# A hybrid decoder layer on Trainium2: building the order of instructions with and without a timed play-through

## The chip, the core and the metric

The kernel runs on one core of a Trainium2 chip. A core has a matrix engine (TensorE, PE in the rows, with its weight loads as PEld), a vector engine (VectorE, DVE), a scalar engine (ScalarE, ACT), a general engine (GpSimd, POOL) and SyncE (SP), which here issues nearly all transfers between the device's memory and the core's. Each engine works through its own list of instructions, and semaphores make one list wait for another. The metric is the device time of one execution in microseconds (us), as the median of several runs.

## The reference, cut to what matters

One layer of a decoder on 2048 prompt tokens and 8 sample tokens, 1024 wide. Two kinds of heads run beside each other between two norms, then an MLP follows.

```python
def _layer(x, states, params):
    h = _rmsnorm(x, norm_pre_mix)
    mix, new_states = _mixer(h, ...)          # h @ w_in, two head groups, o @ w_out
    x = x + _rmsnorm(mix, norm_post_mix)
    u = jnp.square(jax.nn.relu(_rmsnorm(x, norm_pre_mlp) @ w_up))
    return x + _rmsnorm(u @ w_down, norm_post_mlp), new_states

# group A: gated DeltaNet, chunk after chunk (the state S goes from one to the next)
    w_v = triangular_solve(A, bc * vc); w_k = triangular_solve(A, bc * exp(G) * kc)
    def step(S, xs):
        U = wv_ - wk_ @ S
        o = eg_ * (q_ @ S) + qk_ @ U
        return ge_ * S + ke_.T @ U, o
# group B: mLSTM, chunk after chunk (C, n and the running maximum m go on)
        num = w_prev * (q_ @ C) + (P * qk_) @ v_
        h = num / max(|den|, exp(-mt))
        C = w_prev_end * C + (p_end * k_).T @ v_
```

The outputs of both groups are normalised, gated, put side by side and multiplied with w_out. All states come back too.

## The kernel before, in words

The 2048 prompt tokens are worked on in four segments of 512 (the 8 sample tokens ride with the second, whose matmuls are 260 columns wide instead of 512). Each segment goes through the input projection (w_a, 28 units), the mixer, the output projection (w_o), two norms and the MLP (w_up, w_dn). Everything is float32. A product is made from three passes: weights and activations are split into a high and a low part, and hi x hi (L195), hi x lo (L196) and lo x hi (L200) are added in one PSUM bank (tile bk). A unit of weights is a Half, 128 x 512 numbers: SP loads it (L171, tile wraw, four buffers), ACT casts the high part (L178, tile whl, three buffers), DVE subtracts to get the low part (L183), PE runs 12 matmuls on it, and ACT or DVE takes the bank away.

The mixer is a chain of small steps that go between engines. One half of a segment's DeltaNet part (gdn_half, two chunks) does this: transposes (L520, L529) with squares on ACT (L525, L531), products of q and k (L563), a row-by-row solve on DVE (L596, L598) between two trips through memory, then for each chunk PE L618, ACT copies L622, PE L627, DVE L631 and L632, PE L636, ACT L638, PE L643, DVE L645; then for each chunk PE L655, DVE L658, PE L663, ACT L665 (tile W, one buffer), PE L672 with DVE L675 for the next state, PE L680 and L681 for the output, squares on ACT (L684), DVE L685, a power on POOL (L224), the scaling on ACT (L690) and the transposes of the result (L702 in out_T), which go to memory as dO. The mLSTM chunk (ml_chunk, four a segment) is a like chain: L718, L737, L746 and L747, L755, L764, L702, L770. Before the output projection, b_prep reads dO back (L1099). The means of the norms are made by squares on ACT (L1140), additions on POOL (L1141), a matmul (L1153), a power on POOL and a matmul that spreads the result (L1166).

The program writes the wide matmuls in a fixed list and lets the mixer and the norms run beside them: play() keeps an account of wide work and takes a step of such a stream (up to its next yield) when the account allows:

```python
            h.go(part)
            if streams:
                state["due"] += h.cost() * state["rate"]
                while streams and state["due"] > 0:
                    state["due"] -= step()
```

That is the program's order. It isn't yet the order on the engines: the framework (tile) takes every instruction with its place in the program as its priority (split() of a Half gets 300 places ahead of its own), plays the program through on a model of the core, and gives each engine the ready instruction with the best priority at that moment; buffers of a pool are handed out in the same play. What is not ready then is passed by what is. The result is a fixed list for each engine. In the kernel before, the model plays with an estimated time for each instruction (schedule_with_timeline_sim=True, L1586), so an instruction that must wait for another engine is passed by as many others as fit into the estimated wait. The mixer's steps, the splits and the loads all get their places in this way.

## Time and profile before

| what | value |
|---|---|
| median of 3 runs | 2667.09 us (2652.25 to 9010.13) |
| the profiled execution, its own time | 2654.11 us |
| span from its first to its last instruction | 2652.3 us |
| PE busy | 2599.9 us (98%) |
| DVE, ACT, POOL busy | 1727.5, 1283.5, 433.3 us (65%, 48%, 16%) |
| mean clock granted to PE | 0.996 of full speed |
| chain that ended last | PE 88%, DVE 4%, DMA 4%, issue 2%, ACT 1% |
| moved | 377.40 MB, mean 142 GB/s |

Busy times are sums over the span of one execution. A wait is idle time of an engine together with what ended it. The chain that ended last is followed back from the last instruction, at each step to what released it. Busy time of PE is modelled at its ends, so neighbouring matmuls overlap in it and a duration of one is taken from the distance of rows.

### The profile page before, as it was taken

To read this page: it belongs to the slowest core of one execution; us is meant where nothing else is said; L and a number is where in the kernel's file an instruction comes from. 1 tells how busy PE (TensorE), PEld (TensorE's weight loads), DVE (VectorE), ACT (ScalarE), POOL (GpSimd) and SP (SyncE) were. 2 spreads that over 40 slices of the span, in tenths; PEclk is the share of its full clock that TensorE was granted. 3 is DMA by queue.
4 is the path that set the end of the run, shared out by engine and by line. 5 is a ranking of instruction groups with operands and counts; after the bars stand their busy time and mean duration, and the time that the engine had idled before them with its cause. 6 is when DMAs were issued, how large, how long until landed. Compare 5 with 4: busy or idle time off the path is not lost.

```text
span 2652.3 us, 44344 instructions
## 1 busy us (share of the span) xinstructions
PE 2599.9 (98%) x15912; PEld 2268.5 (86%) x15912; DVE 1727.5 (65%) x3513; ACT 1283.5 (48%) x3120; POOL 433.3 (16%) x494
## 2 busy tenths in 40 slices
PE   8999999999999999999999999999999999999998
PEld 6879999787888788878899999997787888788887
DVE  7665758647747656774775766577758566765445
ACT  5636557435536345653655444466354355433332
POOL 2101112311000000530100000054000003552002
PEclk9999999999999999999999999999999999999999
DMA  5444457654324345754433343455333346565222
GB/s 173 155 147 144 151 152 222 207 156 134 108 92 126 96 141 167 236 186 135 139 97 110 107 141 119 138 173 163 99 112 112 106 144 205 182 197 147 93 96 84
DMA packets 292221, 377.40 MB, mean 142 GB/s; under 512 B 42325, under 2 KB 147785, under 8 KB 291993
## 3 DMA queue, kind: packets, MB, share of 16 engines
q1 hardware_dynamic: 289312, 365.13, 44.2%
q0 software_dynamic: 2688, 9.44, 1.3%
q8 instruction: 126, 2.06, 0.3%
q14 instruction: 95, 0.77, 0.1%
HBM read 314.04 MB, written 60.53 MB: 141 GB/s over the span
## 4 chain that ended last, share of the span: by engine, by line
PE 88%; DVE 4%; DMA 4%; issue 2%; ACT 1%; POOL 0%; SPq 0%; DVEq 0%; ACTq 0%; POOLq 0%
PE bk L195 26%; PE bk L196 26%; PE bk L200 26%; DMA wraw<-w_o 1%; DVE whl L183 1%; DVE nt L1214 1%; DMA xt<-x_prompt 1%; DVE X L1218 1%; DMA xt<-dO 1%; PE mx L563 1%; PE mx L655 1%; PE mx L770 1%; PE mx L680 1%; PE mx L681 1%; PE mx L747 1%
## 5 line engine op out<-in xcount | busy, mean ns | idle before, releaser
L178 ACT CAST whl<-wraw 128x512 fp32r<-128x512 f32 x872 | 539.4, 620 | 933.7 <-PE bk L200 866.3
L183 DVE TENSOR_TENSOR whl<-wraw,whl 128x512 fp32r<-128x512 f32 (+1 forms) x872 | 636.3, 732 | 447.5 <-ACT whl L178 433.3
L195 PE MATMUL bk<-Y,whl 128*128 128x512 f32 (+2 forms) x2208 | 733.9, 347 | 4.2 <-ACT whl L178 2.0
L196 PE MATMUL bk<-Y,whl 128*128 128x512 f32 (+2 forms) x2208 | 732.1, 346 | 0.0
L195 PE MATMUL bk<-X,whl 128*128 128x512 f32 (+3 forms) x2024 | 654.9, 340 | 7.2 <-ACT whl L178 7.1
L196 PE MATMUL bk<-X,whl 128*128 128x512 f32 (+3 forms) x2024 | 653.5, 339 | 2.7 <-DVE X L1218 2.5
L200 PE MATMUL bk<-Y,whl 128*128 128x512 f32 (+2 forms) x2176 | 488.2, 344 | 6.9 <-DVE whl L183 6.9
L195 PEld LDWEIGHTS bk<-Y,whl 128*128 128x128 f32 x2208 | 416.2, 189 | 58.9 <-ACT whl L178 3.4
L196 PEld LDWEIGHTS bk<-Y,whl 128*128 128x128 f32 x2208 | 416.9, 189 | 50.4
L200 PE MATMUL bk<-X,whl 128*128 128x512 f32 (+3 forms) x2024 | 442.4, 339 | 8.9 <-DVE whl L183 8.8
L195 PEld LDWEIGHTS bk<-X,whl 128*128 128x128 f32 x2024 | 381.8, 189 | 50.5 <-ACT whl L178 9.5
L196 PEld LDWEIGHTS bk<-X,whl 128*128 128x128 f32 x2024 | 381.7, 189 | 47.5 <-DVE X L1218 4.1
L200 PEld LDWEIGHTS bk<-Y,whl 128*128 128x128 f32 x2176 | 359.1, 189 | 59.5 <-DVE whl L183 8.6
L200 PEld LDWEIGHTS bk<-X,whl 128*128 128x128 f32 x2024 | 326.3, 188 | 54.3 <-DVE whl L183 11.5
L1262 DVE TENSOR_TENSOR acc<-acc,bk 128x512 f32<-128x512 f32 (+2 forms) x296 | 164.3, 557 | 157.3 <-PE bk L200 153.4
L1141 POOL TENSOR_TENSOR NQ<-NQ,nt 128x256 f32<-128x256 f32 (+4 forms) x145 | 143.3, 991 | 470.5 <-ACT nt L1140 464.1
L1251 DVE TENSOR_TENSOR tB<-tB 128x512 f32<-128x512 f32 (+1 forms) x160 | 96.9, 608 | 44.1 <-ACT Y L1250 43.1
L305 DVE SCALAR_TENSOR_TENSOR tB<-tA,cw,tB 128x512 f32<-128x512 f32 x144 | 108.0, 750 | 13.6 <-ACT tB L301 9.3
L1252 DVE TENSOR_TENSOR Y<-tB,Y 128x512 fp32r<-128x512 f32 (+1 forms) x160 | 98.0, 615 | 3.2
L596 DVE TENSOR_TENSOR W<-xt 32x30 f32<-32x30 f32 (+14 forms) x240 | 76.2, 317 | 22.3 <-DMA xt<-dn 17.5
L1249 ACT ACTIVATE tB<-bk 128x512 f32<-128x512 f32 (+1 forms) x160 | 81.8, 511 | 16.1 <-PE bk L200 13.0
L1250 ACT ACTIVATE Y<-tB 128x512 fp32r<-128x512 f32 (+1 forms) x160 | 87.2, 549 | 4.3
(397 smaller groups left out, 2481.8 us busy)
## 6 DMA issues: line engine op xcount, KB each, us to landing
wraw<-w_dn SPq DMA_DIRECT2D x264, 256.0 KB, 2.8
wraw<-w_up SPq DMA_DIRECT2D x256, 256.0 KB, 2.8
wraw<-w_a SPq DMA_DIRECT2D x224, 256.0 KB, 2.9
wraw<-w_o SPq DMA_DIRECT2D x128, 256.0 KB, 3.3
dqkv<-tB SPq DMA_DIRECT2D x48, 256.0 KB, 3.3
gb<-drb SPq DMA_DIRECT2D x32, 256.0 KB, 3.8
qk<-dqkv SPq DMA_DIRECT2D x16, 512.0 KB, 5.7
dzo<-tB SPq DMA_DIRECT2D x32, 256.0 KB, 3.3
```

The costliest lines, as they stand in the source:

```text
L178: A.copy(self.hl[:, 0], self.raw)
L183: V.tensor_tensor(lo, raw, hi.bitcast(F32), op=ALU.subtract)
L195: PE.matmul(o, lhsT=w, rhs=acts[:, k, 0, c0:c1], start=(self.first and k == 0), stop=False)
L196: PE.matmul(o, lhsT=w, rhs=acts[:, k, 1, c0:c1], start=False, stop=(self.packed and self.last and k == 3))
L200: PE.matmul(o, lhsT=w, rhs=acts[:, k, 0, c0:c1], start=False, stop=(self.last and k == 3))
L305: V.scalar_tensor_tensor(acc, pre[:, t:t + SEG], cw[:, j, t:t + 1], acc, op0=ALU.mult, op1=ALU.add)
L1141: G.tensor_tensor(total[:, c0:c1], total[:, c0:c1], sq[:, c0:c1], op=ALU.add)
L1249: A.activation(r[:, :n], p[:, :n], AF.Relu)
L1250: A.activation(sl[:, 0, c0:c1], r[:, :n], AF.Square)
L1251: V.tensor_tensor(r[:, :n], r[:, :n], r[:, :n], op=ALU.mult)
L1252: V.tensor_tensor(sl[:, 1, c0:c1], r[:, :n], sl[:, 0, c0:c1].bitcast(F32), op=ALU.subtract)
L1262: V.tensor_tensor(a, a, p[:, :c1 - c0], op=ALU.add)
```

## The change

The order is no longer built by playing the program through with estimated times; the framework's own play is used, which has no such estimates of how long an instruction takes. Every instruction of the program and its priority stay.

```diff
-    with tile.TileContext(nc, schedule_with_timeline_sim=True) as tc, ExitStack() as ctx:
+    with tile.TileContext(nc) as tc, ExitStack() as ctx:
         program(tc, ctx, d, T)
```

What this moves is seen in the lists of the engines. The first place is PE in the mixer of the second segment (mixer(1)), the steps L618 to L636 of a second chunk. In rows, bk, X and Y belong to the wide matmuls (whl is the weight, and a row without a count stands for one), mx is a bank of the mixer. Before:

```order
L618 MATMUL mx_8233<-Xd_118,NQ_7552 32x32 x8
L195 MATMUL bk_8721<-Y1_7900,whl_8678 128x512
L196 MATMUL bk_8721<-Y1_7900,whl_8678 128x512
L195 MATMUL bk_8721<-Y1_7900,whl_8678 128x512
L196 MATMUL bk_8721<-Y1_7900,whl_8678 128x512
L195 MATMUL bk_8721<-Y1_7900,whl_8678 128x512
L196 MATMUL bk_8721<-Y1_7900,whl_8678 128x512
L195 MATMUL bk_8721<-Y1_7900,whl_8678 128x512
L196 MATMUL bk_8721<-Y1_7900,whl_8678 128x512
L200 MATMUL bk_8721<-Y1_7900,whl_8678 128x512 x4
L195 MATMUL bk_8771<-Y1_7900,whl_8716 128x512
```

Seven more wide matmuls follow before L627. The change:

```order
L618 MATMUL mx_8233<-Xd_118,NQ_7552 32x32 x8
L200 MATMUL bk_8477<-X0_4529,whl_8408 128x512
L195 MATMUL bk_8477<-X1_4530,whl_8472 128x512
L627 MATMUL mx_8263<-Yd_120,P1_122 32x32
L196 MATMUL bk_8477<-X1_4530,whl_8472 128x512
L627 MATMUL mx_8263<-Yd_120,P1_122 32x32 x7
L195 MATMUL bk_8477<-X1_4530,whl_8472 128x512
L196 MATMUL bk_8477<-X1_4530,whl_8472 128x512
L195 MATMUL bk_8477<-X1_4530,whl_8472 128x512
L196 MATMUL bk_8477<-X1_4530,whl_8472 128x512
L195 MATMUL bk_8477<-X1_4530,whl_8472 128x512
L196 MATMUL bk_8477<-X1_4530,whl_8472 128x512
```

L627 has moved from behind 20 wide matmuls to behind two and three; L636 (two rows further on, after one more wide matmul) stands behind seven wide matmuls, where it stood behind 22.

The second place is the output step of a chunk, on PE and on ACT, in the same mixer. On PE before (the L681 that makes the output stands 32 wide matmuls ahead of this piece's L702, with the next chunk's L655 among them):

```order
L200 MATMUL bk<-X_4530,whl 128x512 x4
L195 MATMUL bk<-X_4529,whl 128x512
L196 MATMUL bk<-X_4529,whl 128x512
L195 MATMUL bk<-X_4529,whl 128x512
L196 MATMUL bk<-X_4529,whl 128x512
L195 MATMUL bk<-X_4529,whl 128x512
L196 MATMUL bk<-X_4529,whl 128x512
L663 MATMUL mx<-vt,Yd 128x128 x4
L702 MATMUL mx<-ident,on 128x128 x4
L195 MATMUL bk<-X_4529,whl 128x512
```

PE with the change, from the last L681 on:

```order
L681 MATMUL mx<-W,NQ 128x128
L655 MATMUL mx<-S,qk 128x128 x4
L200 MATMUL bk<-X_4529,whl 128x512 x3
L663 MATMUL mx<-vt,Yd 128x128 x2
L200 MATMUL bk<-X_4529,whl 128x512
L663 MATMUL mx<-vt,Yd 128x128 x2
L702 MATMUL mx<-ident,on 128x128 x2
L195 MATMUL bk<-X_4530,whl 128x512
L196 MATMUL bk<-X_4530,whl 128x512
L702 MATMUL mx<-ident,on 128x128
L195 MATMUL bk<-X_4530,whl 128x512
L702 MATMUL mx<-ident,on 128x128
```

The transposes L702 of the finished chunk stand behind four steps of the next chunk's L655 and four wide matmuls; the last of them is one wide matmul further on, and L672 after it. On ACT before, the end of the squares, then L690:

```order
L684 ACTIVATE junk,so<-mx 128x128
L1250 ACTIVATE Y_8998<-tB 128x512
L684 ACTIVATE junk,so<-mx 128x128
L551 CAST xs<-qk 128x1024
L178 CAST whl<-wraw 128x512
L690 ACTIVATE on<-mx,fac 128x128 x4
L178 CAST whl<-wraw 128x512
L1249 ACTIVATE tB<-bk 128x512
L1250 ACTIVATE Y_8998<-tB 128x512
L665 COPY W<-mx 128x512
```

On ACT with the change:

```order
L665 COPY W<-mx 128x512
L684 ACTIVATE junk,so<-mx 128x128 x4
L690 ACTIVATE on<-mx,fac 128x128 x2
L178 CAST whl<-wraw 128x512
L690 ACTIVATE on<-mx,fac 128x128 x2
L665 COPY W<-mx 128x512
L551 CAST xs<-qk 128x1024
L684 ACTIVATE junk,so<-mx 128x128 x4
```

L690 has moved up to the squares that it depends on (by way of DVE and POOL), and L665 of the next chunk stands right behind it.

The third place is SP at the end of the last segment's mixer: L704 writes the last piece of dO, L1099 reads dO back for the output projection, L171 loads weights, the L10xx lines write final states. Before:

```order
L699 DMA on<-dzo_140 128x4x128
L171 DMA wraw<-w_o 128x512 x2
L1084 DMA o_pconv<-gb 36x128
L704 DMA dO_144<-on 128x4x128
L171 DMA wraw<-w_o 128x512 x2
L1099 DMA xt<-dO_144 128x2x256 x2
L171 DMA wraw<-w_o 128x512 x3
L1182 DMA xt<-xT 128x4x256 x2
```

The change:

```order
L1084 DMA o_pconv<-gb 36x128
L704 DMA dO_144<-on 128x4x128
L171 DMA wraw<-w_dn 128x512 x5
L171 DMA wraw<-w_up 128x512 x8
L171 DMA wraw<-w_dn 128x512 x8
L171 DMA wraw<-w_up 128x512 x8
L171 DMA wraw<-w_dn 128x512 x6
L1099 DMA xt<-dO_144 128x2x256 x2
```

Between the write and the read of dO there were two loads of weights; now there are 35.

## Rows read from the trace of the kernel before

**Rows 1.** Page, part 1: busy us, share of the span, instructions of each engine.

```profile
PE 2599.9 (98%) x15912; PEld 2268.5 (86%) x15912; DVE 1727.5 (65%) x3513; ACT 1283.5 (48%) x3120; POOL 433.3 (16%) x494
```

**Rows 2.** Busy time by stretch: stretch, its us, busy of PE, PEld, DVE, ACT, POOL, clock.

```profile
0.00:50.00 50.00, 38.62 (x206) 32.98 (x207) 33.50 (x88) 30.37 (x64) 11.32 (x32) 1.00 0.56 190
427.00:510.00 83.00, 77.15 (x509) 68.89 (x508) 66.87 (x146) 53.66 (x125) 28.34 (x26) 0.99 0.70 217
660.00:1000.00 340.00, 340.00 (x1780) 278.46 (x1779) 217.80 (x477) 160.40 (x411) 16.36 (x20) 1.00 0.37 113
2190.00:2300.00 110.00, 100.72 (x629) 89.27 (x629) 74.60 (x115) 60.97 (x133) 44.97 (x46) 0.98 0.64 194
```

**Rows 3.** What PE waited for: us in total, times, longest us.

```profile
PE bk L200 <- DVE whl L183: 15.7, 14, 2.7
PE bk L195 <- ACT whl L178: 9.1, 12, 1.4
```

**Rows 4.** Timeline inside a mixer: start us, us, engine, line, operation, count, idle before.

```profile
182.74 0.43 PE L618 MATMUL mx<-Xd,NQ 32*32 32x32 f32 x14
...
183.21 0.54 ACT L622 COPY P<-mx 32x128 f32<-32x128 f32 x2 [2.45 <-PE mx L618]
...
187.92 0.44 PE L627 MATMUL mx<-Yd,P 32*32 32x32 f32 x16
...
189.04 0.30 DVE L632 STREAM_TRANSPOSE Xd<-Yd 32x128 f32<-32x128 f32 x1
```

**Rows 5.** Timeline, the output step of one chunk (L681 to L690).

```profile
942.82 0.28 ACT L684 ACTIVATE junk<-mx 128x128 f32<-128x128 f32 x1 [2.75 <-PE mx L681]
...
944.74 1.01 POOL L224 TENSOR_TENSOR fac<-so,mhalf 128x4 f32<-128x4 f32 x1 [22.05 <-DVE so L685]
...
945.88 1.14 ACT L690 ACTIVATE on<-mx,fac 128x128 f32<-128x128 f32 x4
```

**Rows 6.** Chain that ended last, in order of time, 935 to 985: start us, us, what.

```profile
935.69 0.93 PE bk L200 x4
...
940.11 0.89 PE mx L672 x8
...
951.56 0.44 PE mx L702 x4
```

**Rows 7.** Groups by line: busy us, mean ns of one, idle before it.

```profile
L183 DVE TENSOR_TENSOR whl<-wraw,whl 128x512 fp32r<-128x512 f32 (+1 forms) x872 | 636.3, 732 | 447.5 <-ACT whl L178 433.3 <-DMA wraw<-w_up 2.6 <-DMA wraw<-w_dn 2.1
...
L178 ACT CAST whl<-wraw 128x512 fp32r<-128x512 f32 x872 | 539.4, 620 | 933.7 <-PE bk L200 866.3 <-DMA wraw<-w_o 24.0 <-issue 8.3
...
L525 ACT ACTIVATE junk<-kt 128x128 f32<-128x128 f32 x64 | 19.9, 311 | 1.7
...
L531 ACT ACTIVATE junk<-mx 128x128 f32<-128x128 f32 x64 | 17.8, 278 | 1.5
...
L531 ACT ACTIVATION_READ_ACCUMULATOR junk<-mx 128x1 f32 x64 | 12.7, 198 | 0.0
```

**Rows 8.** The same view, POOL's additions of squares.

```profile
L1141 POOL TENSOR_TENSOR NQ<-NQ,nt 128x256 f32<-128x256 f32 (+4 forms) x145 | 143.3, 991 | 470.5 <-ACT nt L1140 464.1 <-ACT sab L850 2.9 <-DMA xt<-dx 0.9
```

**Rows 9.** Busy time by stretch around some of PE's waits; PEclk stands after the engines.

```profile
508.00:514.00 6.00, 5.49 (x17) 4.19 (x17) 4.70 (x4) 4.36 (x9) 5.76 (x4) 0.72 1.03 312
2194.00:2201.00 7.00, 4.37 (x37) 4.16 (x36) 2.15 (x5) 2.15 (x6) 0.00 (x0) 1.00 0.53 98
2201.00:2207.00 6.00, 6.00 (x40) 6.00 (x40) 2.00 (x4) 2.08 (x5) 0.00 (x0) 0.72 0.93 272
2207.00:2220.00 13.00, 11.62 (x96) 11.22 (x96) 7.69 (x10) 8.15 (x20) 4.00 (x5) 1.00 0.73 242
262.00:275.00 13.00, 11.65 (x97) 11.44 (x96) 9.01 (x27) 7.93 (x23) 2.98 (x3) 1.00 0.65 192
```

**Rows 10.** Chain that ended last, whole span: transfers at two hand-overs.

```profile
427.07 2.92 DMA dO<-on
...
2199.85 2.42 DMA dO<-on
...
2202.28 4.12 DMA xt<-dO
```

## The prediction, made before the changed kernel was run

> **What bounds the kernel now.** I read four views. The page's busy shares come first [rows 1]: PE is busy 2599.9 of the 2652.3 us of the profiled execution, so all its waiting is 52 us; DVE is busy 65%, ACT 48%. An order can only add to or take from those 52 us. Then busy time by stretch [rows 2]: the reader is to see that PE waits at the start (50.00 - 38.62 = 11.4 us) and where one segment hands over to the next (427 to 510: 5.9 us; 2190 to 2300: 9.3), and not at all while a mixer runs beside the wide matmuls (660 to 1000: 340.00 of 340.00). Third, what PE waited for [rows 3]: mostly the weight split (L183 on DVE, L178 on ACT), 25 us together. Last, the timeline within a mixer [rows 4, 5], which shows what the old order bought: slack behind every step of the chain.
>
> **What the change moves.** No instruction is added or removed on any engine that computes; the same 14,815 matmuls stand in another order, so the sum is a sum of waits. A wide matmul (512 columns, called H here) takes 0.93 / 4 = 0.233 us, one of 128 columns 0.89 / 4 = 0.22 us [rows 6]. In the old order a mixer step that needs another engine's answer stands 20 to 30 H behind the step before it (20 H = 4.7 us); in the new one 3 to 8 H (0.7 to 1.9 us). The old order hid every answer with room to spare, the new one has hardly any room. Is that enough?
>
> Steps within a mixer. L618 ends at 182.74 + 0.43 = 183.17; ACT's two copies (L622) end at 183.75: the answer takes 0.58 us, and PE came back for it only at 187.92, 4.2 us late on purpose [rows 4]. The new order leaves 3 H = 0.70 us: just enough. L627 ends at 188.36, L631 and L632 on DVE end at 189.34: 0.98 us; the new order leaves 7 H = 1.63: enough. So with a free ACT and DVE these steps cost 0, and save 0 too, since PE did other matmuls meanwhile. They cost what the answering engine is still busy with. Six answers by ACT and six by DVE stand in the chain of half a segment (the DVE ones are L632, L658 and L675, each twice, the ACT ones L622, L638 and L665), 96 in the eight halves. A cast of 0.62 us on an engine that is busy 48% makes an answer late by 0.48 x 0.31 = 0.15 us on average, a split of 0.73 us at 65% by 0.24 [rows 1, 7]; I take 0.12 of the mean of 0.20, since part of it falls into the room left: 96 x 0.12 = 12 us. Bounds: 0, and 96 x 0.68 = 65 us if each answer met a whole cast or split.
>
> The output step (the second place in the change's section). From the end of L681 (942.78; ACT starts at 942.82), four squares (L684) and L685 on DVE come before the POOL power, which ends at 945.75, and L690 gives its four heads from 945.88 to 947.02 [rows 5]. The first head is ready about 3.4 us after L681, the fourth 4.24. In the old order PE asks for them (L702) at 951.56, 8.8 us after L681 [rows 6]. In the new order the first of the pair in a half is asked after L655 x4 (0.89), 3 H (0.70), L663 x2 (0.44), 1 H (0.23) and L663 x2 (0.44): 2.7 us, and 2.4 beside the 260-column matmuls: 0.7 to 1.0 short, eight times, 6.8 us. The second comes after 10 H = 2.33 us or a little more: 1.0 short in six halves, 0.1 in two: 6.2. Of the 16 mLSTM chunks, whose chain has the same parts, five are short, 4.5 in all. That is 17 us. In the new order ACT has L665, which the next L672 needs, behind L690, so that answer is held too; most of it lies within the wait already counted, 2 us more. Bounds: 0 if L690 is early everywhere, and 32 x 1.8 = 58 if ACT also puts a cast (0.62) and L665 (0.59) in between at every place.
>
> Single places. At the second half of the first mixer the 16 transposes (L520, L529) and the 12 L563 now stand without a matmul of the projections between them (13 before). ACT's squares behind the transposes are 8 x (0.311 + 0.198) + 8 x (0.278 + 0.198) = 7.9 us against 16 x 0.22 = 3.5 us of PE; a part may go on later, since only the last ones hold a bank: 3.5 us, between 0 and 4.4 [rows 7]. At the ends of the last two segments L1153, which sums what POOL added up (0.99 us an addition, eight in a chain, 8 us [rows 8]), stands up to 4 us earlier than its chain; but PE waited in that stretch before too (2190 to 2300 [rows 2]), so I take 4 of the 8 us counted. At the start the first weight matmul now waits for 24 transposes, where before 17 were enough: 2 us. The gate and solve chains have smaller ones, 4 together.
>
> What is gained. In the old order the mixer's tail ends so late that its write of dO and the read of it (L1099) lie on the chain that ended last, at 427 and at 2200 to 2206 [rows 10]. In the new order the last L702 stands some 400 H earlier at the first of these and 500 H at the second, and there SP has 35 weight loads between the write and the read (third place). PE's waits there go: 2194 to 2201 lost 2.6 us, 2207 to 2220 lost 1.4, and between them the clock was at 0.72 of full speed for 6 us, 1.7 us more [rows 9]. That is 6 us with a little at 427. The rest of the hand-overs stays: its waits come from the norms' work on DVE, which is as long as before.
>
> The sum: 12 + 17 + 2 + 3.5 + 4 + 2 + 4 - 6 = 38.5 us. The profiled execution took 2654.11 us (a span of 2652.3 and 1.8 around it); the median of the runs shown, 2667.09, is 0.5% above it, the lowest 2652.25. 2654 + 38 = 2692 us, 1.4% over the profiled one, 0.9% over the median. About 2%, some 53 us, is what a measurement of this kernel can tell from no change.
>
> **The clock.** [...] It stayed at 1.00 in 262 to 275 with 1.35 us of waiting [rows 2, 9]. The new waits are single ones of 0.7 to 1.5 us between full matmuls, so I add nothing for it. [...]
>
> **Rivals.**
> First, slower by over 2%: ACT's queue, with L690 at its head waiting for POOL, holds what is behind it, and a mixer's later answers come late in a row. In the new order L684, L690, L665 and the next L684 stand with only a cast and L551 between them. If each of the 32 output steps costs 1.8 us instead of 0.55 and the 96 steps 0.3 instead of 0.12, that is 58 + 29 = 87 in place of 31: 2654 + 38 + 56 = 2748. It decides from a mean of 1.2 us per output step with 0.2 per step, 2720 us. For it: all slack is gone, so each disturbance is paid; against it: ACT is free 52% of the time, and the stretches of 340 us show no wait that grows. Chance 0.27. [...]
> Second, the chain costs nothing and the gain is real: waits within half a mixer are absorbed by the split's three buffers, as all waits before were. 12 + 17 + 2 become 5, the single places 5 in place of 13.5: 2654 + 10 - 6 = 2658, and 2640 if the start and the norms gain as well. Chance 0.15.
> Third, the clock falls after the output steps: 32 falls of 1.7 us are 54, 2692 + 54 = 2746. Against it is the window at 262. Chance 0.05.
> Faster by over 2% would need 2614 us or less, which leaves PE some 12 us of waiting in all, where the start alone costs 11 [rows 1, 2]. Chance 0.02.
> The forecast itself, waits of 20 to 60 us net: 0.51.
>
> **How the numbers follow.** The likeliest case gives 2692 us. Its own range goes from 2670 to 2715. The range that is to hold the time takes in most of the second rival and the cheaper half of the first: 2650 to 2738; outside lie the faster case, the best of the second rival and the worst of the first and third. Slower by over 2% is the first and third rival with a little of the forecast's upper end, less their cheap ends: 0.32. Faster 0.02, within 2% 0.66.
>
> **What the new profile would show.** Right: PE's busy time about 2600 again; new waits of PE for ACT L690 (at L702) and for ACT L665, L622 or DVE L632, L658 of 0.1 to 1.5 us each, most of 30 us in all; windows of the mixer stretches at 96 to 98% where they had 100%; the xt<-dO reads gone from the chain that ended last. Wrong: if the waits of PE still list only the splits, the steps are covered and the second rival holds. If single waits are over 2 us, or L690's group shows casts late behind it and PE waiting for L178 more than the 9 us of now [rows 3], the first holds. If the mean clock falls below 0.98, the third.

## The result and the profile after

| | before | changed |
|---|---|---|
| median of the runs, us | 2660.38 | 2743.49 (2741.65 to 2745.20) |
| the profiled execution, its own time, us | 2654.11 | 2745.20 |
| span, us | 2652.3 | 2743.5 |
| mean granted clock | 0.996 | 0.988 |

The changed kernel takes 1.0324 times as long as the kernel before, 95% interval [1.0296, 1.0352]: 3.2% slower, where 1.4% over the profiled execution was forecast, and 5 us above the upper end of the range. The four runs of the kernel before took 2652.25, 2653.67, 2667.09 and 9010.13 us; the ratio leaves the last one out. The changed kernel's own lines follow; the first fence is part 1 of the page (the answer to [rows 1]) and the clock of the core.

```profile
PE 2636.6 (96%) x15912; PEld 2284.0 (83%) x15912; DVE 1720.5 (63%) x3513; ACT 1285.0 (47%) x3120; POOL 413.6 (15%) x494
```
```profile
core 0: 2743.5 us, clock 0.988
```

DVE, ACT and POOL are busy about as long as before or less. PE's wait is 2743.5 - 2636.6 = 107 us where it was 52, and its busy time is up by 37 us with the same instructions. So idle time alone will not account for the 91 us between the two spans.

What PE waited for in the changed kernel (us in total, times, longest), against [rows 3]:

```profile
PE mx L1153 <- POOL NQ L1141: 19.3, 6, 5.2
PE mx L702 <- ACT on L690: 12.4, 15, 1.2
PE mx L702 <- ACT on L764: 11.8, 8, 3.0
PE bk L200 <- DVE whl L183: 10.9, 11, 3.6
...
PE mx L1166 <- POOL st L224: 5.1, 3, 3.8
...
PE bk L195 <- ACT whl L178: 4.1, 5, 1.1
...
PE mx L618 <- DVE Xd L612: 1.7, 2, 1.2
```

The splits (L183, L178), first before with 25 us, now make 15. In front of them stand two new kinds of wait: the sums of the norms (L1153) for POOL's additions, and the transposes of the output (L702) for ACT's scaling (L690 in the DeltaNet part, L764 in the mLSTM).

Busy time by stretch, the changed kernel (stretch, its us, busy of PE, PEld, DVE, ACT, POOL, clock): the start, then a piece out of each of the four mixers.

```profile
0.00:50.00 50.00, 37.51 (x211) 32.48 (x212) 34.97 (x102) 30.07 (x66) 10.22 (x30) 1.00 0.58 178
100.00:400.00 300.00, 280.94 (x2037) 251.98 (x2036) 198.48 (x523) 164.31 (x501) 29.64 (x47) 0.99 0.49 150
650.00:1000.00 350.00, 344.59 (x1825) 279.01 (x1825) 236.77 (x543) 172.15 (x461) 23.14 (x36) 1.00 0.39 119
1350.00:1650.00 300.00, 295.35 (x2530) 287.88 (x2529) 203.26 (x528) 157.05 (x473) 20.15 (x23) 1.00 0.39 117
1900.00:2150.00 250.00, 245.13 (x1380) 199.29 (x1379) 174.44 (x420) 122.96 (x348) 17.32 (x20) 1.00 0.38 115
```

Mixers two to four stand at 98% where PE had no gap [rows 2], the first at 94%. At the start PE waits 12.5 us, before 11.4.

**Where the 90 us are.** Idle time under-reports, so I compare progress instead: PE runs the same 12,888 wide matmuls in both kernels, with the same numbers of columns in the same sequence, and the start of the k-th one tells how late the kernel is at that point. The lateness gained between two such points is what that stage lost, whatever name the loss has in the profile. The borders lie between mixers and hand-overs (k = 560, 2230, 3300, 4650, 6300, 8700, 9650, 10800, 11400). This is worked out from the profiled execution of each kernel, in us against the profiled execution of the kernel before; the experiments below are in the same table, with short names.

```
kernel                       start  mixer 1  mixers 2-4  hand-overs 1,2  hand-overs 3,4  in all
changed                        1.5     26.8        28.6             2.5            30.4    89.9
x1  mixers timed              -2.0     15.5         5.8             5.7            31.5    56.5
x2  hand-overs timed          -0.1     28.3        29.1            -0.5            -0.8    56.0
x5  PE timed                   0.2      7.4         7.6             1.4             5.6    22.2
x6  the others timed           8.2     50.9        79.0             6.5            12.5   157.1
x10 before, sums early         5.3     -0.5         0.1            -1.6            28.7    32.0
x12 same, waits part filled    2.2      2.3        -0.1             2.1            22.6    29.1
x15 same, all filled           0.1      0.6        -0.1             0.0            16.0    16.6
x3  sums later                -0.4     28.6        28.2             4.5             3.0    63.9
x4  transposes later           1.1     23.2        27.3             0.1            28.0    79.7
x7  ten before output          0.5     30.4        13.9             2.6            30.0    77.4
x8  slower mixers             -0.3     18.1        11.5            -2.5            33.3    60.1
x11 slower mixers, sums later  0.0     22.5        11.4             3.7             3.6    41.2
x9  slower, hand-overs timed   1.6     24.4        11.9            -0.1             5.1    42.9
x13 ten at every step          2.2     30.3        11.0             3.9            38.0    85.4
x14 same, sums late            0.0     31.0         9.5             0.5            15.9    56.9
x16 evictions first            3.2     25.5        32.3             4.1            17.2    82.3
x17 all three                  1.9     28.6         8.8             2.4            10.3    52.0
x18 before, evictions first    2.6      1.3        -0.5            12.4             1.1    16.9
```

So the changed kernel loses 55 us in the mixers and 33 in the hand-overs, nearly all of the latter in the last two, and almost nothing at the start. Each row is one execution: x10, x12 and x15 have the same order at the start and show 5.3, 2.2 and 0.1 us there, so a difference of that size in one column says nothing.

The same stages can be split further: what PE was idle more, what the half clock cost while PE was busy (its busy time there times the missing share of the clock), and what is left, which lies in the distances between the starts of matmuls (us more than in the kernel before; the last hand-over here up to the last instruction).

```
                       later by   idle   half clock   left
mixer 1                  26.8     16.9      1.7        8.2
mixers 2-4               28.6     14.2      0.0       14.4
hand-overs 1,2            2.5      3.2      3.0       -3.7
hand-overs 3,4           31.7     18.6     12.8        0.3
hand-overs 3,4 of x10    28.2     17.4     12.0       -1.2
```

In the last two hand-overs the loss is idle time and half clock and nothing else, in the changed kernel as in x10. In the mixers there is hardly any half clock, and 22.6 us are neither.

**A hand-over.** The timeline of the changed kernel at the third hand-over (start us, us, engine, line, operation, idle before) shows the sum that is asked for too early:

```profile
1820.49 0.42 ACT L1140 ACTIVATE nt<-Y 128x256 f32<-128x256 f32 x1 [0.75 <-POOL NQ L1141]
...
1823.48 1.01 PE L1153 MATMUL mx<-ones,NQ 128*128 128x2 f32 x4 [4.22 <-POOL NQ L1141]
...
1824.35 0.57 PE L195 MATMUL bk<-Y,whl 128*128 128x260 f32 x1
...
1824.71 0.42 PE L196 MATMUL bk<-Y,whl 128*128 128x260 f32 x1
```

While PE stands at L1153, ACT is still making the squares (L1140) that POOL adds up. And when PE goes on, two 260-column matmuls begin 0.36 us apart, then 0.22; before the wait it was 0.12. The windows around it (same columns, clock behind POOL) show why:

```profile
1816.00:1820.00 4.00, 3.16 (x24) 2.95 (x24) 2.88 (x5) 3.56 (x11) 3.11 (x4) 1.00 0.86 267
1820.00:1824.00 4.00, 0.52 (x3) 0.53 (x3) 0.54 (x2) 1.97 (x5) 3.26 (x5) 0.74 0.79 253
1824.00:1828.00 4.00, 4.00 (x20) 4.00 (x20) 1.30 (x4) 0.14 (x1) 0.00 (x0) 0.50 0.24 70
1828.00:1832.00 4.00, 4.00 (x32) 4.00 (x32) 1.62 (x4) 1.32 (x4) 2.17 (x3) 0.91 0.04 7
```

From 1824 to 1828 the clock is at half (0.50 of full speed), after PE has been idle for 4.2 us: 20 matmuls against 32 in the next window, all of it counted as busy.

**An output step in a mixer.** Timeline of the changed kernel, DeltaNet part, the counterpart of [rows 5]:

```profile
894.63 0.39 PE L681 MATMUL mx<-W,NQ 128*128 128x128 f32 x2
...
895.11 0.28 ACT L684 ACTIVATE junk<-mx 128x128 f32<-128x128 f32 x1 [3.10 <-PE mx L681]
...
896.95 1.01 POOL L224 TENSOR_TENSOR fac<-so,mhalf 128x4 f32<-128x4 f32 x1 [6.58 <-DVE so L685]
...
898.00 0.37 ACT L690 ACTIVATE on<-mx,fac 128x128 f32<-128x128 f32 x1 [1.32 <-POOL fac L224]
...
898.42 0.33 PE L702 MATMUL mx<-ident,on 128*128 128x128 f32 x1 [1.10 <-ACT on L690]
```

L681 ends at 895.0, the first head is there at 898.4: 3.4 us, the figure that the prediction had. PE was back 1.1 us too soon. Behind the first head a cast (L178) stands on ACT here, and the other three heads begin only at 898.77.

**What the busy time hides.** The same groups of steps in both kernels, by line and shape (count, busy us, mean ns of one, idle before). First the kernel before, then the changed one:

```profile
L663 PE MATMUL mx<-vt,Yd 128*128 128x128 f32 x128 | 17.8, 274 | 0.0
...
L627 PE MATMUL mx<-Yd,P 32*32 32x32 f32 x256 | 7.0, 194 | 0.0
```
```profile
L663 PE MATMUL mx<-vt,Yd 128*128 128x128 f32 x128 | 22.5, 287 | 0.0
...
L627 PE MATMUL mx<-Yd,P 32*32 32x32 f32 x256 | 10.6, 195 | 0.0
```

One of them takes about as long as it did, and no idle time stands before them, but the groups show 4.7 and 3.6 us more. That is not yet what PE lost: a group's busy time counts what two neighbours of the group share only once (128 of L663 at 274 ns would be 35 us, the group shows 17.8), and when a wide matmul comes between them it shares its time with that one instead. The groups are cut up, L663 into 44 pieces where there were 24, L627 into 31 where there were 16 (one L627, a wide matmul, seven L627, as the change's section shows). Others stand closer together, and the wide matmuls lie in 315 stretches where they lay in 323. The distances from start to start, without idle time, tell more. In the mixers they are 24.2 us longer (1.7 of it half clock), and of this 8.8 lie at L702, in 83 pieces where there were 86, 5.4 at L627 and 1.4 at L663. So 20 more pieces of L663 cost 1.4 us, and cutting up is not the main thing. L702 is where PE asks too early. A transpose of 0.27 us begins 0.11 us behind the one before it in the kernel before, so by an estimate from these two a wait of up to 0.16 us would disappear under the end of the matmul ahead and show no idle time. That the 8.8 us are such waits is likely and not shown.

### The profile page after: what moved, and what is told of

It reads as the page before. It is cut to its first block, busy times and chain, and to the rows that moved or that the text cites. A ratio compares the mean times of both kernels' runs of the same rounds, so it can differ in the third digit from the quotient of the medians.

```text
span 2743.5 us, 44381 instructions
## 1 busy us (share of the span) xinstructions
PE 2636.6 (96%) x15912; PEld 2284.0 (83%) x15912; DVE 1720.5 (63%) x3513; ACT 1285.0 (47%) x3120; POOL 413.6 (15%) x494
## 4 chain that ended last, share of the span: by engine, by line
PE 77%; DVE 7%; issue 5%; POOL 5%; ACT 3%; DMA 3%; SPq 0%; POOLq 0%; ACTq 0%; DVEq 0%
PE bk L195 23%; PE bk L196 22%; PE bk L200 22%; DVE whl L183 2%; POOL NQ L1141 1%; POOL fac L224 1%; ACT whl L178 1%; PE mx L702 1%; DVE nt L1214 1%; ACT junk L684 1%; PE mx L563 1%; DMA xt<-x_prompt 1%; DVE xt L598 1%; DVE W L596 1%; DVE nt L1322 1%
## 5 line engine op out<-in xcount | busy, mean ns | idle before, releaser
L178 ACT CAST whl<-wraw 128x512 fp32r<-128x512 f32 x872 | 538.7, 619 | 973.0 <-PE bk L200 907.8
L183 DVE TENSOR_TENSOR whl<-wraw,whl 128x512 fp32r<-128x512 f32 (+1 forms) x872 | 634.5, 730 | 462.1 <-ACT whl L178 456.9
L195 PE MATMUL bk<-Y,whl 128*128 128x512 f32 (+2 forms) x2208 | 737.9, 349 | 8.7 <-ACT whl L178 3.9
L195 PE MATMUL bk<-X,whl 128*128 128x512 f32 (+3 forms) x2024 | 660.9, 343 | 4.6 <-ACT X L1217 4.3
L200 PE MATMUL bk<-Y,whl 128*128 128x512 f32 (+2 forms) x2176 | 487.3, 345 | 3.6 <-DVE whl L183 3.6
L195 PEld LDWEIGHTS bk<-Y,whl 128*128 128x128 f32 x2208 | 418.4, 190 | 63.0 <-ACT whl L178 5.1
L200 PE MATMUL bk<-X,whl 128*128 128x512 f32 (+3 forms) x2024 | 445.2, 340 | 7.3 <-DVE whl L183 7.3
L195 PEld LDWEIGHTS bk<-X,whl 128*128 128x128 f32 x2024 | 384.6, 190 | 46.6 <-ACT X L1217 5.6
L200 PEld LDWEIGHTS bk<-Y,whl 128*128 128x128 f32 x2176 | 360.4, 190 | 55.7 <-DVE whl L183 4.3
L200 PEld LDWEIGHTS bk<-X,whl 128*128 128x128 f32 x2024 | 328.2, 189 | 53.2 <-DVE whl L183 9.8
L1141 POOL TENSOR_TENSOR NQ<-NQ,nt 128x256 f32<-128x256 f32 (+4 forms) x145 | 133.7, 926 | 831.2 <-ACT nt L1140 683.1
```

What stands on the lines that cost most here:

```text
L178: A.copy(self.hl[:, 0], self.raw)
L183: V.tensor_tensor(lo, raw, hi.bitcast(F32), op=ALU.subtract)
L195: PE.matmul(o, lhsT=w, rhs=acts[:, k, 0, c0:c1], start=(self.first and k == 0), stop=False)
L200: PE.matmul(o, lhsT=w, rhs=acts[:, k, 0, c0:c1], start=False, stop=(self.last and k == 3))
L1141: G.tensor_tensor(total[:, c0:c1], total[:, c0:c1], sq[:, c0:c1], op=ALU.add)
```

## The experiments

In the time of each run stands the kernel before on the same chip; ratios are to that. Several kernels use one device: the program is built twice, the list of each engine is read from the first build, edited or not, and laid on the second as an order. The edges fix the order of issue on one engine and make no engine wait for another.

```diff
+    traced = {i.name: i for i in nc.cur_bb.bb.instructions}
+    for chain in want:                      # one list for each engine
+        for a, b in zip(chain, chain[1:]):
+            tc.add_manual_dep(traced[b], a, mybir.DependencyInfo(
+                mybir.DependencyClass.NoSync, mybir.DependencyReason.DATA), reason="order")
...
+    _, order = build(T, arrays, timed_for_the_order)
+    edit(order)
+    nc, _ = build(T, arrays, timed_for_the_rest, order.values())
```

### Which part of the program: x1 and x2

x1 gives the start and the four mixers the order of the kernel before, on every engine, and leaves the hand-overs to the untimed play; x2 does the reverse. Only the order inside a part is fixed, not how the instructions of two parts stand among each other.

```diff
+PARTS, ENGINES = ('start', 'mix'), ('PE', 'Activation', 'DVE', 'Pool', 'SP')   # x1
+PARTS, ENGINES = ('hand',), ('PE', 'Activation', 'DVE', 'Pool', 'SP')           # x2
```

> On every engine the instructions of the start and of the four mixers stand in the order of the kernel before; those of the hand-overs, norms and projections behind them keep the order of the changed kernel. Theory A (two places share the loss: of the 91 us about 57 come where mixers run and about 35 at the hand-overs): 2743 - 57 = 2686 us, 1.011 times the kernel before. Theory B (the hand-overs lose because the mixers now end early and their work no longer fills the hand-overs; the order inside the mixers matters little): the mixers are late again, so the hand-overs recover as well, under 2670 us. Theory C (almost all is the clock and the sums at the hand-overs): over 2715 us.

> The reverse: the hand-overs, norms and projections behind the mixers stand in the order of the kernel before, the start and the mixers in that of the changed kernel. Theory A: 2743 - 35 = 2708 us (1.020 times before), and the two gains with those of the mixers kernel add up to 91 within 10 us. Theory B: 2735 us or more, since the mixers still end early. Theory C: under 2690 us.

x1: 2711.16 us, 1.0207 [1.0190, 1.0224]. x2: 2711.45 us, 1.0208 [1.0193, 1.0223]. In x2 the loss of the hand-overs goes from 33 to -1 us and the mixers keep theirs (57); in x1 the mixers fall from 55 to 21 and the hand-overs stay (37). The two are separate losses: the gains, 32 each, are 64 of the 85 us between the kernels; the rest is what the mixers keep in x1. Most of that, 15.5 us, is in the first mixer, and there the edit reached only half. In mixers 2 to 4 nearly all steps on PE stand where they stood before. In the first mixer they do so up to the 1711th wide matmul; behind it L663 follows L655 after 9, 9, 5 and 6 wide matmuls, where the kernel before has 24, 24, 27 and 27 and the changed one 6, 7, 5 and 7. All of the 15.5 us come behind the 1610th wide matmul. The forecast had -2 us for all the hand-overs.

### Which engine's order: x5 and x6

x5 lays PE's list of the kernel before on the changed kernel and leaves the other engines to the untimed play. x6 does the reverse: PE's list of the changed kernel, and the others laid out by the timed play around it.

```diff
+ENGINES = ("PE",)
+    _, order = build(T, arrays, True)            # x5: PE's order timed
+    nc, _ = build(T, arrays, False, order.values())
...
+    _, order = build(T, arrays, False)           # x6: PE's order untimed
+    nc, _ = build(T, arrays, True, order.values())
```

> PE's instructions stand exactly in the order of the kernel before; the other engines' order and the buffers come from the play without estimates, which has to follow PE's. Theory A (the loss lies in where PE's own queue asks for an answer): nearly all comes back, 2655 to 2675 us. Rival E (the order in the queues of ACT, DVE and POOL matters by itself, an instruction at a queue's head that waits holds what is behind it): over 2700 us.

> The reverse: PE's instructions stand exactly in the order of the changed kernel, and the queues of ACT, DVE, POOL and SP and the buffers are laid out by the play with estimated times, under that order of PE. Theory A: little comes back, 2725 us or more, with PE still waiting some 20 us or more at L702 and 15 or more at L1153. Rival E: 2710 us or less.

x5: 2679.08 us, 1.0080 [1.0065, 1.0095]. x6: 2811.83 us, 1.0578 [1.0562, 1.0594]. PE's order alone gives back 64 of the 85 us; 2655 to 2675 us had been expected, and 21 us over the kernel before are left for the other engines' order and the buffers. Those two alone don't help: laid out around PE's early asking by the timed play, they cost 68 us more. PE's waits in x6:

```profile
PE mx L702 <- ACT on L690: 35.2, 16, 3.4
PE mx L702 <- ACT on L764: 17.2, 9, 5.5
PE mx L618 <- DVE Xd L612: 15.6, 6, 7.7
```

So the queues of ACT and DVE in the changed kernel are not what is bad about it. With PE asking as early as it does, they give the answers earlier than the timed play's do (12.4 us of waits at L702 for L690 against 35.2).

### The hand-overs: x10, x12, x15 and x3

x10 injects the suspected cause into the kernel before: its order on every engine, but the ten groups of L1153 that the untimed play has earlier stand where the changed kernel has them, 12 to 41 wide matmuls ahead of their old place.

```diff
+    late = [i for i in order["PE"] if kinds.get(i) in MOVED]       # MOVED = ("sum",)
+    early = [i for i in late if there[i] < here[i]]                # by wide matmuls ahead of it
...
+            while k < len(early) and there[early[k]] <= n:
+                got.append(early[k])
```

> The kernel before, with its order on every engine, and one thing altered: the ten groups of row sums (L1153) that the change had moved forward on PE stand where the changed kernel has them, 12 to 41 wide matmuls earlier. Theory A (that place alone brings the wait for POOL's additions, and the wait brings the half clock): 15 to 20 us of waits at L1153 and some 15 us of half clock, part of it in place of waits that were there: 2658 + 28 = 2686 us, mean clock 0.990. Rival D (PE has to wait for the norm's chain somewhere in any case): waits move from L195 and L200 to L1153, the clock stays at 0.996 and the time below 2668 us.

2683.27 us, 1.0101 [1.0086, 1.0116]: 27 us from ten moved groups. Hand-overs 3 and 4 lose 14.1 and 14.6, the mixers nothing. PE's waits, the timeline at the longest wait, and windows during and after it:

```profile
PE mx L1153 <- POOL NQ L1141: 17.6, 5, 5.6
```
```profile
1804.93 7.25 POOL L1141 TENSOR_TENSOR NQ<-NQ,nt 128x260 f32<-128x260 f32 x8 [0.33 <-ACT nt L1140]
...
1812.23 2.85 PE L1153 MATMUL mx<-ones,NQ 128*128 128x2 f32 x14 [5.55 <-POOL NQ L1141]
```
```profile
1806.00:1812.00 6.00, 0.68 (x3) 0.20 (x2) 2.39 (x3) 2.83 (x8) 5.53 (x8) 0.76 0.81 258
1812.00:1820.00 8.00, 7.77 (x27) 6.71 (x28) 1.21 (x2) 1.75 (x4) 0.18 (x1) 0.54 0.10 33
```

Eight additions in a chain of 7.25 us end at 1812.2, and PE has been standing for 5.55 us; then the next 8 us run at 0.54 of full speed. That is a second price of the same wait. x12 and x15 take it apart. They are x10 with matmuls that compute nothing (identity times identity into the bank that the sum then overwrites) put ahead of four of the sums: x12 has 12 at each, x15 has 24 at the two longest waits, so that PE is not idle though the sum is as late as before.

```diff
+            for _ in range(fill):
+                PE.matmul(p[:, 0:128], lhsT=ident, rhs=ident, start=True, stop=True)
```

> The kernel with the sums early (2683 us), on every engine in the same order, with one addition: ahead of four of the ten groups of sums, those that stand where PE waited 3.2 to 5.9 us, PE gets 12 more matmuls of 128 columns, whose result nobody reads and which the sums' own first write covers (12 x 0.22 = 2.6 us, shorter than each wait, so they take no time of their own). In that kernel the clock was at half for about 3, 4, 2 and 4 us' worth of lost work right behind these four waits. Theory G (the waiting is what lowers the clock, so work in its place keeps it): the waits' ends stay, the half clock goes: 2683 - 12 = 2671 us, mean clock 0.994 or more. Rival H (the clock falls for another reason, the small sums or the load of the chip at the hand-overs): 2680 us or more and the clock at 0.989.

> The kernel with early sums and filled waits (2678 us), with 24 matmuls in place of 12 at the second and fourth place, where a wait of 2.9 and 3.5 us was left and the clock still fell. 24 take 5.7 us, about as long as the whole waits there (5.9 and 5.4 us). Theory G (the rest of the wait lowered the clock): no half clock at the two places, 2678 - 7 = 2671 us. Rival H: the clock falls there as before, 2678 us or more.

x12: 2677.68 us, 1.0083 [1.0069, 1.0098], not to be told from x10 by itself. Its 12 matmuls take 2.84 us; at the two places where that covered the wait, the clock stayed at 1.00, at the other two 2.9 and 3.5 us of wait were left and it fell (0.58 and 0.57 over the 8 us behind). x15: 2671.28 us, 1.0063 [1.0046, 1.0080]. Its clock, and a window that takes in the place of the longest wait and the 12 us behind it:

```profile
core 0: 2668.4 us, clock 0.997
```
```profile
1800.00:1820.00 20.00, 19.80 (x118) 17.14 (x118) 9.19 (x16) 9.21 (x20) 8.01 (x10) 1.00 0.40 133
```

The clock is that of the kernel before, and 12 of the 27 us are back. The other 15 are the waits as such (17.6 us in x10). The mean clock is 0.989 in x10, 0.993 in x12 and 0.997 in x15, though nobody uses what the added matmuls compute.

x3 takes the cause out of the changed kernel: L1153 and L1166 get a priority of 80 places later in the program.

```diff
-                for k, total in enumerate(totals):
-                    PE.matmul(p[:n, 2 * i:2 * i + 2], lhsT=total[:, c:c + n], ...
+                with tc.high_priority(-80):
+                    for k, total in enumerate(totals):
+                        PE.matmul(p[:n, 2 * i:2 * i + 2], lhsT=total[:, c:c + n], ...
```

> The changed kernel, with only the matmuls of the row sums (L1153) and of the spread behind them (L1166) put 80 places later in priority, which sets most of them some 20 to 60 wide matmuls later on PE. Theory A (PE asks for the sums before POOL's additions are done, and the clock falls after each such wait): the 20 us of waits at L1153, 5 at L1166 and about 20 us of half clock behind them go, less a few that come back further on: 2743 - 38 = 2705 us, mean clock 0.995. Rival D (the norm's chain on DVE and POOL is itself too long, so that whatever needs its result next waits instead): waits move to L195 behind X, the clock stays at 0.988 and the time above 2730 us.

2727.39 us, 1.0264 [1.0247, 1.0280]; the hand-overs fall from 33 to 7 in the profiled execution (2722.49 us, the fastest), and 16 us are gained in the median, where 38 had been expected. One gain is given back at the very end, where nothing is left to run ahead of the sums and they are late: `PE mx L1154 <- ACT on L1267: 4.7, 1, 4.7` (lines moved by one or two). One fixed number of places doesn't suit every sum. The cause is shown by x2, x3 and x10 alike: taken out by either way the loss goes, put in alone it comes (28.7 of the 30.4 us in the last two hand-overs).

### The mixers: x4, x7, x8 and x13

x4 ties each group of L702 behind a later wide matmul (34, 28 or 8 on), in the untimed play.

```diff
+            t = PE.transpose(p[:, h * 128:(h + 1) * 128], on[:, h], ident)
+            late.append([t, 34 if s == 0 else 28 if base == 0 else 8])
```

> The changed kernel, with only the transposes of the finished chunks (L702) issued 17 or more wide matmuls later on PE; ACT's queue is not touched on purpose. Theory A (PE asks too soon for what L690 or L764 gives): the 30 us of long waits at L702 and 3 of short ones go: 2743 - 33 = 2710 us. Rival E (ACT's queue is the cause: L690 stands at its head and holds the answers behind it, so PE waits at L672, L627 or for the casts L178 instead): at least half of it comes back there, 2725 us or more.

2742.18 us, 1.0318 [1.0298, 1.0337]: no difference. It decides nothing, because the play let the steps behind move along, and the distance to the output step hardly grew (7 wide matmuls stayed 7, 18 became 23); 15 us of waits at L702 were left. x7 sets the distance by hand: ten wide matmuls more ahead of each group of L702, everything else on PE with the same distances as in the changed kernel.

```diff
+        if kinds.get(n) == "out":
+            if outs % 4 == 0:
+                shift += COVER           # COVER = 10
```

> The changed kernel's order on PE, with one difference: ahead of each group of L702 ten more wide matmuls are put between the chunk's last L681 or L747 and its L702, and all that follows in the same mixer moves back by ten as well, so that every other distance on PE stays (the median from L681 to L702 goes from 8.5 wide matmuls to 18.5, from L747 to L702 from 23.5 to 33.5). The run in which the transposes were only given a later place left most of these distances as they were (7 and 7, 18 and 23), since the steps behind them moved along, so it decided nothing. Ten wide matmuls are 2.3 us, 1.2 us of 260 columns. Theory A: the waits at L702 fall from 24 us to 3 or less, 2743 - 28 = 2715 us. Rival E (L690 in ACT's queue holds the answers behind it whatever PE does): they come back at L672, L627 or behind L178, 2730 us or more.

2731.72 us, 1.0278 [1.0260, 1.0295]. The waits at L702 fall from 24.2 us to 2.6, and 12 come back, where 28 had been expected; the time is that of rival E (2730 or more). Part of the rest is found one step on, where the changed kernel had 2.5, 1.7 and less than 0.4 us:

```profile
PE mx L416 <- DVE gl L412: 6.1, 3, 4.3
...
PE mx L618 <- DVE Xd L612: 3.6, 5, 1.4
PE mx L672 <- ACT W L665: 3.4, 4, 1.5
```

Mixers 2 to 4 lose 13.9 us instead of 28.6, the first 30.4 instead of 26.8. So in the later mixers half of the loss was missing room ahead of L702, and what rival E foretold (the waits come back at L672) is a small part. x8 makes room everywhere by asking less of the play: the mixer's pace is 1.2 steps' worth of work for 2.1, and 1.0 for 1.6.

```diff
-    main.append(rate(2.1))
+    main.append(rate(1.2))
...
-            main.append(lambda s=s: stream(mixer(s + 1)))
-            main.append(rate(1.6))
+            main.append(lambda s=s: stream(mixer(s + 1)))
+            main.append(rate(1.0))
```

> The changed kernel with one thing altered in the program: the mixers are paced more slowly among the wide matmuls (rate 1.2 in place of 2.1 in the first segment, 1.0 in place of 1.6 in the others), so that every hop of the chain gets more of them between (the median from L618 to L627 goes from 2 wide matmuls to 7.5, from L655 to L663 from 3 to 12, from L681 to L702 from 8.5 to 24, from L747 to L702 from 23.5 to 36). The hand-overs' order stays. Theory A with what the run with ten more at L702 taught (there 24 us of waits went and only 12 us were gained, since the next hops, short as they were, took over part): with room at every hop the mixers give back most of their 57 us: 2743 - 45 = 2698 us, L702's waits under 4 us and no other line of the mixers over 4. Rival F (the mixers' loss is queueing on ACT and DVE behind the casts and splits, whatever the room): 2725 us or more.

2721.99 us, 1.0251 [1.0234, 1.0268]: mixers 30 us instead of 55 (2 to 4: 11.5; the first: 18), hand-overs 3 and 4 unchanged. 2698 had been expected; 10.6 us of waits at L702 are left, 8.7 of them in the first mixer. There the slower pace reaches the first half only: L663 follows L655 after 24 wide matmuls in it, but after 5 to 7 in the second half, as in the changed kernel, and all of the first mixer's 18 us come behind the 1610th wide matmul. x13 puts ten more wide matmuls ahead of every step of the mixers on PE:

```diff
+        shift += COVER if mixer and new else 0       # at each step behind a wide matmul
```

> The changed kernel's order on PE with ten more wide matmuls ahead of every piece of mixer work that followed a wide matmul, in all four mixers (from the first L520 to the last L702), so that no hop is left as it was: L618 to L627 12 of them at least (before the change 20, with it 2), L655 to L663 13, L681 to L702 20, L747 to L702 19; the mixers still end before the hand-overs (the last chunk's transposes stand behind 1.7 of 2.2 thousand wide matmuls in the first). Theory A (the mixers' loss is room at the hops and nothing else): from the first to the last mixer the 55 us fall under 8, the hand-overs keep their 33: 2743 - 48 = 2695 us. Theory J (the first mixer, which kept 15 to 30 us in every run that left the other engines' queues to the play without estimates, loses by something else): it keeps 15 us or more, 2707 us or more. Rival F (queueing whatever the room): 2725 us or more.

2741.62 us, 1.0325 [1.0308, 1.0343]. Mixers 2 to 4 lose 11.0, but the first as much as before (30.3), and hand-overs 3 and 4 lose 38 instead of 30: the last mixer's tail (25 of its matmuls) now stands behind the border and counts there. Theory A's 2695 us is missed and theory J's 2707 or more holds; the time fits rival F too, but in mixers 2 to 4 room does take off more than half, which F denies. In the first mixer a new wait stands, this time of the projection for its own bank:

```profile
259.08 0.53 ACT L301 ACTIVATE tB<-bk,cw 128x260 f32<-128x260 f32 x1
...
259.65 0.59 PE L195 MATMUL bk<-Y,whl 128*128 128x260 f32 x1 [5.26 <-ACT tB L301]
```

From 243 to 258 ACT had some 40 squares and scalings of the mixer (L525, L531, L581, L582) in its list ahead of L301, which takes the projection's bank away.

### Both causes together, and a theory that fell: x9, x11, x14, x16, x17 and x18

x9 is x8 with x2's hand-overs, x11 is x8 with x3's late sums, x14 is x13 with the sums (and the spreads L1166) at the places that the kernel before has.

> The slower pace of the mixers, and the hand-overs in the order of the kernel before. If both places are what the change cost, 2711 (the hand-overs alone) - 45 = 2666 us, within 1% of the kernel before. It would beat that kernel (under 2650 us) only if the mixers' early end, which leaves no wait at 2150 to 2300 in the changed kernel where the one before lost 14 us, came on top. Rival F: 2690 us or more.

> The slower pace of the mixers and the row sums 80 places later, both in the order without estimates: two small edits of the program in place of the play with estimated times. If the gains add (45 for the pace, 16 as measured for the sums): 2743 - 61 = 2682 us, 0.9% over the kernel before. If they overlap at the hand-overs, up to 2700 us.

> The same ten at every hop, and the sums (L1153) and the spread (L1166) of the hand-overs at the places that the kernel before has for them, 12 to 50 wide matmuls later. If these two are the whole of the loss: 2695 - 26 (what later sums gave at the hand-overs in the trace of that run) = 2669 us. Below 2650 us, so faster than the kernel before, if the early end of the mixers is a gain that stays. With theory J 2681 us or more.

x9: 2698.09 us, 1.0157 [1.0142, 1.0173]. x11: 2694.22 us, 1.0147 [1.0132, 1.0162]. x14: 2713.68 us, 1.0221 [1.0205, 1.0236]. x9 and x14 miss what had been expected (2666 and 2669) by 32 and 45 us, x11 lies between its 2682 and 2700. The two remedies do not get in each other's way: x8's 21 us and x3's 16 would make 37, x11 gains 49. With two edits of numbers in the program it is the best untimed kernel found, 38 us behind the one before. x9 has its own new wait, 9.3 us of L195 for X L1101, the read back of dO at the first hand-over: a slower mixer ends later. The largest part that stays in each is mixer 1, at 22 to 31 us; the time of x9 is also the one that rival F gave (2690 or more).

x16 and x17 tried the reason that x13's timeline suggests for it: the evictions of the projection (done) get 300 places of precedence, so that no work of the mixer on ACT or DVE stands ahead of them; x16 in the changed kernel, x17 in x14. x18 does the same to the kernel before.

```diff
-                self.done(self.parts)
+                with tc.high_priority(300):
+                    self.done(self.parts)
```

> The changed kernel with one thing altered: the evictions of the wide matmuls' banks (what runs when a unit is done, as L300 and L301 or L1249 and L1262) get the priority that the splits have, 300 places ahead. In the run with ten at every hop PE waited 5.3 us in the first mixer for L301, which stood on ACT behind some 40 of the mixer's squares and scalings. Theory K (in the first mixer the evictions stand behind the mixer's work on ACT and DVE): from the first mixer's 27 us some 10 go, the other places stay: 2743 - 10 = 2733 us. Rival (what PE waits for in the changed kernel itself are the mixer's answers, and evictions in front of them only delay them): 2743 us or more.

> Ten at every hop, late sums and spread, and the evictions 300 places ahead. The run without the last had 2714 us, 31 of its 57 us over the kernel before in the first mixer. Theory K: the first mixer's loss falls to 12, 2714 - 19 = 2695 us. Rival (another cause in the first mixer): 2710 us or more.

> The kernel before, played with estimated times, with the evictions 300 places ahead: the version with the best chance to beat both. Its waits are mostly for the splits (25 us), and an eviction in front of a norm's or a mixer's instruction frees a bank sooner, but delays the norms at the hand-overs by as much: 2650 to 2665 us, no difference that can be told. Faster than 2640 us only if banks, not splits, were what PE lacked; slower than 2680 us if the norms' chain is what counts.

x16: 2743.31 us, 1.0343 [1.0316, 1.0369], mixer 1 at 25.5. x17: 2708.77 us, 1.0212 [1.0190, 1.0234], mixer 1 at 28.6. x18: 2669.76 us, 1.0055 [1.0035, 1.0075], slower than the kernel before; PE now waits 24.2 us at L200 for the splits where it was 15.7 [rows 3]. Theory K falls with x16 (2733 expected) and gets little from x17 (2695 expected, 5 us gained): the wait at L301 is real where it stands, and it is not what mixer 1 loses most of its time by. No kernel that was run beat the one before.

## Why the prediction was off

**The time.** 2692 us was forecast, 2743 measured, above the 2738 that the range ends at. The count of 14,815 matmuls is wrong (the trace of either kernel has 15,912 on PE), but only their being the same is used. "PE's busy time about 2600 again" failed by 37 us.

**The direction and the place in the mixers held.** The forecast had waits of PE at L702 for ACT as the largest new item; in the mixers they are, with 24.2 us against 17. Its parts: the DeltaNet output steps 6.8 + 6.2 = 13 us forecast, 12.4 measured in 15 waits of at most 1.2 (0.7 to 1.0 forecast); L690's answer 3.4 us after L681, as in the row above. The mLSTM chunks 4.5 us forecast, 11.8 measured in 8 waits: here "whose chain has the same parts" was wrong. The two longest of these waits lie on the chain that ended last of the changed kernel (start us, us, what); this is the first of them:

```profile
321.82 4.22 DMA gb<-drb
326.18 0.64 POOL E L493
326.82 0.99 POOL fac L224
...
328.04 0.38 ACT on L764
328.46 0.33 PE mx L702
```

The power on POOL (L224) had its input from DVE at 324.9; it begins at 326.8, because L493, the mask of the next chunk's decay, stands ahead of it in POOL's list and waits for a read of gb, which has one buffer. In 3 of the 16 mLSTM chunks L224 begins 1.6 to 1.9 us late in this way, 5.2 us in all; in the kernel before it is never over 0.4. The prediction looked for such a queue on ACT and not on POOL. This is read from the trace; no run took it apart.

**The 96 steps within the mixers: 12 us forecast, nearly nothing of it as a wait.** Of the kind named (L627, L636, L663, L672 for ACT and DVE) no line above 0.4 us is in the list; L618 has 1.7. But the mixers lost 55 us by the table, with 31 us of idle time: the sum was made of waits, by "the sum is a sum of waits", and that sentence is the step that failed here. It put 12 + 17 + 2 + 3.5 + 4 = 38.5 us into the mixers (the start's 2 and the hand-overs' -2 make nothing together), not far from the idle time; 1.7 us are a fall of the clock in the first mixer, and 22.6 us more are in the distances between matmuls, of which L702 has 8.8 and L627 5.4. If those of L627 are short waits for ACT's copies (L622), the 12 us were not for nothing; no run tells.

**The hand-overs: -2 us forecast, 33 measured.** This is the larger miss, 35 of the 51 us between the sum (38.5) and the table (89.9). The step is "L1153 ... stands up to 4 us earlier than its chain; but PE waited in that stretch before too, so I take 4 of the 8 us". L1153 has 19.3 us of waits in 6 places, up to 5.2 each. The waits that the stretch had before did not pay for the new one: idle time in the last two hand-overs rose by 18.6 us. The second part of the step is "I add nothing" for the clock. For the mixers that was nearly right: the half clock cost 1.7 us there, at 231 to 235 behind a wait of 2.51 us for an eviction (L323 on ACT). The 3.0 us wait at 328 leaves it at full speed, as the windows before and after its end show.

```profile
322.00:329.00 7.00, 4.00 (x35) 3.69 (x33) 2.13 (x10) 3.18 (x16) 1.76 (x3) 1.00 0.72 206
329.00:333.00 4.00, 4.00 (x32) 3.79 (x31) 3.07 (x8) 4.00 (x14) 0.00 (x0) 1.00 0.24 70
```

But the waits of L1153 weren't in the sum, so neither was the half clock that begins in three of them (4.22, 5.16 and 4.65 us). In all it cost 12.8 us in the last two hand-overs, part of that behind waits of 1.92 to 3.52 us, and it is 12 of x10's 27 us (x15).

**The gain of 6 us.** The reads of dO at the last two hand-overs (2199 to 2206 in [rows 10]) are gone from the chain that ended last, as forecast; the first is still on it (359.34, 2.79 us, xt<-dO). What that gave can't be told apart from the larger loss there. The start cost 1.5 us against 2 forecast; runs with one and the same start differ by more.

**The rivals.** The time is near the first rival's 2748 us, and its mechanism is not what happened. One of its signs came by the letter, single waits over 2 us (L764 3.0, L1153 5.2), but not where it looked: those for L690 are at most 1.2, and PE's wait for L178 fell from 9.1 to 4.1 instead of rising. x5 and x6 tell the same: with PE's old order and ACT's list left to the untimed play 64 of the 85 us are gone, and with ACT's list laid out again under PE's new order the kernel is slower still. The second rival (nothing lost) is refuted by every mixer window. The third expected the clock to fall after output steps; it falls in the hand-overs, once in a mixer, never behind an output step, and the mean of 0.988 is above its sign of 0.98. Both bounds of the output step (0 and 58 us) were far off; the first head came as quickly as in the row of before.

**Still open.** Mixer 1 keeps 15 to 31 us (51 in x6) in every kernel in which PE's list there is not wholly that of the kernel before, and 7 with all of it and the other engines untimed (x5). x1 and x8, where it keeps 15.5 and 18, left its second half as tight as the changed kernel has it, and the loss lies there, so they are no sign of another cause. But in x13, x14 and x17 every hop has room and 29 to 31 us stay: in x13 17 of idle time, 7 of half clock and 6 of distances, with waits at L702 (8.4 us), at L301 (5.3) and in the gates (L416 and L433, 4.5). Its wide matmuls of 260 columns, which give half as much room each (0.12 us from start to start, against 0.23 with 512 columns), are not the reason by themselves: the third mixer has only such ones beside it and loses 9.3 of the 28.6. Mixer 1 differs from it in the pace (2.1 against 1.6) and in standing beside the input projection and not the MLP. Evictions first took off 1 and 2 us (x16, x17), which is no more than executions differ. Which of its steps would need how much room was not found.

## What to carry to other kernels

Before an order that was built with estimated times is replaced by one that has none, list the answers that the matrix engine waits for, with the longest chain behind each, and look first at the slow chains outside the dense loop: here the sums of eight additions on POOL (7.25 us at x10's longest wait), the powers behind them (1.01 us for L224), the reads back of a result (2.79 us for xt<-dO at 359). Look for the price of such waits in two places: x10, which moves nothing but the sums, has 17.4 us of idle time more in the last two hand-overs, and besides that 12.0 us of half clock. Compare progress at fixed points of the work (the k-th wide matmul), since idle time showed 31 of the 55 us that the mixers lost. And before a remedy is judged by what is left, see in the trace which part of the list it reached.

## What the runs showed of the hardware that was not expected

The half clock outlasted the wait that brought it: after a wait of 4.2 us the 4 us behind it ran at 0.50, after one of 5.55 us the next 8 at 0.54. The length of a wait alone didn't tell whether it came. In the changed kernel a wait of 2.51 us that ended at 230.3 was followed by half clock, and in the kernel before one of 2.63 us that ended at 2200.5 ([rows 9]); waits of 3.00 us (ending at 328.5) and 2.47 us (at 341.2) in the changed kernel were not.

```profile
230.30 0.39 PE L195 MATMUL bk<-Y,whl 128*128 128x260 f32 x1 [2.51 <-ACT tB L323]
```
```profile
232.00:236.00 4.00, 4.00 (x25) 4.00 (x24) 0.35 (x1) 0.62 (x1) 0.01 (x1) 0.66 0.66 190
```

Matmuls without use in that place kept the clock at 1.00 (at two of four places in x12, in x15's window of 1800 to 1820) and cost nothing, since PE would have stood there: x15 is 12 us faster than x10, though it has 72 matmuls more (12 at two places, 24, or 5.52 us, at the two others).

The lists of the other engines mattered in the direction opposite to the one that I expected. ACT's and DVE's lists in the changed kernel look careless, with L690 at the head of ACT's queue while POOL works; laid out anew by the timed play around the same PE list, buffers included, they cost 68 us more (x6), with the longest wait at L702 growing from 3.0 to 5.5 us and a wait of 7.7 us at L618.
